# How many raw weight tiles may be held: a fixed number for each mode, or the pages that each unit leaves free

## The chip, the cores and the metric

The kernel runs on one core of a Trainium2 chip. The metric is the device time of one execution in microseconds (us), taken as the median of several runs. Engines are named as in the profile: PE is the matrix engine (PEld its weight loads), DVE the vector engine, ACT the scalar engine, POOL the general engine, SP the engine that only issues transfers; a q behind a name means its sequencer or its queue.

## The reference, cut to what matters

The kernel computes one layer over 256 positions of width 2048, all in float32: a SwiGLU feed-forward block, a mixer, a second feed-forward block, and a gated input at the end, with a layer norm behind each of the first three.

```python
def _swiglu(x, w1, w3, w2):
    return (jax.nn.silu(x @ w1) * (x @ w3)) @ w2
...
    merged = jax.nn.sigmoid(ga) * (y_m @ w_up_m) + jax.nn.sigmoid(gb) * (y_sb @ w_up_sb)
    return merged @ w_out
...
    for i in range(DEPTH):
        x = _layer_norm(ALPHA * x + 0.5 * _swiglu(x, ffn1_w1[i], ffn1_w3[i], ffn1_w2[i]), ln1_g[i], ln1_b[i])
        mix = _hybrid_mixer(x, w_in[i], b_gates_m[i], conv_m[i], norm_m[i], w_up_m[i], w_up_sb[i], w_out[i])
        x = _layer_norm(ALPHA * x + mix, ln2_g[i], ln2_b[i])
        x = _layer_norm(ALPHA * x + 0.5 * _swiglu(x, ffn2_w1[i], ffn2_w3[i], ffn2_w2[i]), ln3_g[i], ln3_b[i])
        x = x + jax.nn.sigmoid(x @ w_ple_gate[i]) * (p[i] @ w_ple_proj[i])
```

In the mixer, `ga` and `gb` (the two branch gates), the mLSTM's inputs and the attention's inputs are columns of one product `x @ w_in`. Nearly all the time is in these matrix products: 256 rows against weights that are read from memory once.

## The kernel before, in words

**Weights.** A weight tile is 256 rows by 512 columns, 512 KB. It is loaded by SP as a raw tile of one page (128 partitions, 2 x 512 float32). Then it is split into two float32r halves, of one page each: ACT casts it (hi, line 1277), DVE subtracts the cast from it (lo, line 1281). PE needs three matmuls for each product: activation hi by weight hi (line 1333), hi by lo (1334), lo by hi (1335). A **unit** is one weight tile against 128 positions, six matmuls.

**Seven products.** Where two column blocks of weights meet the same input, `seven` (line 356) replaces the eight block products of a 2 x 2 by 2 x 2 scheme by seven, with sums of weight tiles. A sum is made in the raw tile itself, by DVE (`plus`, line 373) or by a second transfer that adds to what is there (`plus_load`, line 379, issued by POOL). Such an adding transfer can start only when the raw tile has landed and the split of its earlier content has read it. One pair of column blocks has 28 units and 16 raw tiles; the four raw tiles b11 are held from the first units to the last, since each is changed three times.

**Order of work.** `program` is a list of units written out in advance; `weave` (line 168) mixes a main row of plain units with a side row of seven-product units. In each feed-forward block nine of the eleven column chunks are on the side; in the mixer there are six pairs: one for the attention's values, one for a gate of the mLSTM, and four for the branch gates (lines 1114 to 1115, `pair(g)`), which write into `gt` (line 1097). The main row there goes from the attention inputs over `half(0, 0)` and `half(1, 0)` (up-projection of the mLSTM branch, w_up_m) to the part called late (line 1112), which begins with `half(0, 1)` (attention branch, w_up_sb). The products of `half` end in line 1073. `Sched` runs the small work (transposes, activations, attention steps) at due times between the units.

**Pages.** One pool of 51 pages (`PAGES`) holds raw tiles, splits and nearly everything else: residuals (`big`, line 228), transposed activations (`act_tile`, line 231), attention tiles. A new tile takes the page of an earlier one, and its first writer waits until the last reader of that earlier tile is through.

**How far ahead.** The loop over `program` (line 1315) emits a unit, lets the small work run, and calls `splits_due` (line 1292), which emits the split of the next weight as long as fewer splits than the mode's second number are held. Each split gives back the raw tiles that it was the last to need, and `loads` (line 1242) then issues further raw loads as long as fewer than the mode's first number are held:

```python
HELD = {"ffn": (11, 6), "mix": (6, 6), "woven": (9, 6), "wide": (11, 6), "late": (8, 5)}
```

The mode "ffn" holds in the feed-forward blocks, "woven", "wide" and "late" in the woven part of the mixer one after the other, "mix" elsewhere. Within 6 weights of a stage boundary the numbers are 4 and 11. These are counts in the order of emission; SP, ACT, DVE and PE work through their own lists, so that SP can be well ahead of the splits that were emitted before its loads.

Of the kernel before, what the change touches and what calls it, by code (L numbers as in the profile page):

```python
# [24 lines left out]

PAGES = 51
TEMP_BUFS = 6


HELD = {"ffn": (11, 6), "mix": (6, 6), "woven": (9, 6), "wide": (11, 6), "late": (8, 5)}  # L30
RAW_EDGE, SPLIT_EDGE = 4, 11
EDGE = 6

# [1 line left out]
PSUM_BUFS = 8  # L35
# [151 lines left out]
    return [p[0] for p in pairs] + [p[1] for p in pairs]  # L187


@with_exitstack  # L190
def kernel(
    ctx: ExitStack,
    tc: tile.TileContext,
    x, p, ffn1_w1, ffn1_w3, ffn1_w2, ln1_g, ln1_b, w_in, b_gates_m, conv_m, norm_m,
    w_up_m, w_up_sb, w_out, ln2_g, ln2_b, ffn2_w1, ffn2_w3, ffn2_w2, ln3_g, ln3_b,
    w_ple_gate, w_ple_proj, out,
):
    nc = tc.nc
# [4 lines left out]
    consts = ctx.enter_context(tc.tile_pool(name="consts", bufs=1))  # L203
    dram_pool = ctx.enter_context(tc.tile_pool(name="dram", bufs=1, space=bass.MemoryType.DRAM))
    page_pool = ctx.enter_context(tc.tile_pool(name="page", bufs=PAGES))
    temp_pool = ctx.enter_context(tc.tile_pool(name="temp", bufs=TEMP_BUFS))
    small = ctx.enter_context(tc.tile_pool(name="small", bufs=4))
    ps_pool = ctx.enter_context(tc.tile_pool(name="ps", bufs=PSUM_BUFS, space=bass.MemoryType.PSUM))
    ctx.enter_context(tc.manual_schedule())

    sched = Sched()
    temps = [0]
# [49 lines left out]
    def load_x(c, t):  # L262
        nc.sync.dma_start(out=xres(t, c * COL), in_=x[t * P:(t + 1) * P, c * COL:(c + 1) * COL])
# [844 lines left out]
    last = sb(14, 15)  # L1108
# [3 lines left out]
    late = [Mode("late")] + half(0, 1, True) + half(1, 1, True) + ups(2)  # L1112
# [126 lines left out]
    def pieces(j):  # L1239
        return [slice(0, 1), slice(1, 2)] if j == 0 else [slice(0, 2)]  # L1240

    def loads(most=len(raws)):
        while pos["load"] < most and pos["raw"] < (4 if pos["at"] < 6 else limits(pos["split"])[0]):
            j = pos["load"]
            r = raws[j]
            r.tile = page_pool.tile([P, 2, COL], F32, name="raw", tag="page")
            for ks in pieces(j):
                at = 0
                for src in r.src:
                    n = src.shape[-1]  # L1250
                    nc.sync.dma_start(out=r.tile[:, ks, at:at + n], in_=src[:, ks])
# [16 lines left out]
    def split_one():  # L1268
        j = pos["split"]
        w = weights[j]  # L1270
        make(j)
        assert w.made or not w.make
        r = w.raw.tile[:, :, :w.cols]
        splits[j] = [page_pool.tile([P, 2, COL], F32R, name="split", tag="page") for _ in range(2)]
        hi, lo = (h[:, :, :w.cols] for h in splits[j])
        for ks in pieces(j):
            nc.scalar.copy(hi[:, ks], r[:, ks])  # L1277
# [3 lines left out]
            nc.vector.tensor_tensor(out=lo[:, ks], in0=r[:, ks], in1=hi[:, ks], op=ALU.subtract)  # L1281
        pos["split"] += 1
        for f in w.soon:
            assert f.raw.tile is not None
            f.make()
            f.made = True
        pos["raw"] -= len(w.frees)
        for r in w.frees:
            r.tile = None
        loads()  # L1290

    def splits_due():
        most = pos["at"] + 3 if pos["at"] < 8 else len(weights)
        while pos["split"] < most and len(splits) < limits(pos["split"])[1]:
            split_one()
            if at_edge(pos["split"]):
                break

    for c in range(4):
        if c == 0:  # L1300
            load_x(0, 0)
            loads(1)
        for t in range(TT):
            if c:
                load_x(c, t)
            sched.spawn(start(c, t), max(0.01 * t, 5.2 * c + 1.3 * t - 2.6))
        loads(2 * c + 2)
    sched.run()
    split_one()
    sched.now = 0.02  # L1310
    sched.run()
    splits_due()
    warm(WARM2)
    make_tri()
    for u in program:
        if isinstance(u, (Boundary, Mode)):
            continue
# [12 lines left out]
        for k in range(2):  # L1330
            hi, lo = a[:, 0, u.sub + k], a[:, 1, u.sub + k]
            first, last = u.start and k == 0, u.stop and k == 1
            nc.tensor.matmul(ps, hi, w[0][:, k, :u.cols], start=first, stop=False, skip_group_check=u.onto)  # L1333
            nc.tensor.matmul(ps, hi, w[1][:, k, :u.cols], start=False, stop=False, skip_group_check=u.onto)  # L1334
            nc.tensor.matmul(ps, lo, w[0][:, k, :u.cols], start=False, stop=last, skip_group_check=u.onto)  # L1335
# [35 lines left out]
```

## Time and profile before

| what | us |
|---|---|
| median of 3 runs | 2166.78 |
| lowest, highest of them | 2165.8, 2167.62 |
| the profiled execution | 2172.74 |
| its span, first to last instruction | 2171.1 |
| PE busy in it | 2154.1 |
| DVE busy | 1921.2 |
| ACT busy | 1360.8 |

The profile shows one execution. Busy time of PE is the union of its matmuls, whose ends are modelled, so small losses between matmuls lie inside it; idle time of PE is what is left of the span. A row of the windows view gives one stretch: its length, then busy time and number of instructions of PE, PEld, DVE, ACT and POOL, the granted clock of PE, the share of the DMA engines' time in use, and GB/s. A row of the waits view names who sat idle, what ended it, the total, the number of times and the longest. A number in brackets at the end of a timeline row is the idle time just before it, and what ended it.

### The profile page before, as it was taken

To read this page: it belongs to the slowest core of one execution; us is meant where nothing else is said; L and a number is where in the kernel's file an instruction comes from. 1 tells how busy PE (TensorE), PEld (TensorE's weight loads), DVE (VectorE), ACT (ScalarE), POOL (GpSimd) and SP (SyncE) were. 2 spreads that over 40 slices of the span, in tenths; PEclk is the share of its full clock that TensorE was granted. 3 is DMA by queue.
4 is the path that set the end of the run, shared out by engine and by line. 5 is a ranking of instruction groups with operands and counts; after the bars stand their busy time and mean duration, and the time that the engine had idled before them with its cause. 6 is when DMAs were issued, how large, how long until landed. Compare 5 with 4: busy or idle time off the path is not lost.

```text
span 2171.1 us, 27709 instructions
## 1 busy us (share of the span) xinstructions
PE 2154.1 (99%) x9774; PEld 1778.0 (82%) x9774; DVE 1921.2 (88%) x2122; ACT 1360.8 (63%) x1681; POOL 227.8 (10%) x194
## 2 busy tenths in 40 slices
PE   9999999999999999999999999999999999999999
PEld 7888888888888888888877888888888888887887
DVE  6899999999998898889889886799999999999974
ACT  7656666656665766678876563655656666556572
POOL 0111111111100000101110100011111111110000
PEclk9999999999999999999999999999999999999999
DMA  9899899999994667998988986679999999999642
GB/s 348 215 276 270 249 270 273 277 273 265 276 316 134 218 218 215 239 254 244 286 238 210 303 296 206 203 193 270 270 246 271 279 274 272 251 271 291 238 158 94
DMA packets 285355, 540.16 MB, mean 249 GB/s; under 512 B 17272, under 2 KB 34592, under 8 KB 285216
## 3 DMA queue, kind: packets, MB, share of 16 engines
q1 hardware_dynamic: 234624, 440.87, 59.8%
q0 software_dynamic: 50592, 97.53, 25.1%
q8 instruction: 76, 1.25, 0.2%
q14 instruction: 63, 0.52, 0.1%
HBM read 532.04 MB, written 6.29 MB: 248 GB/s over the span
## 4 chain that ended last, share of the span: by engine, by line
PE 87%; DVE 5%; DMA 3%; issue 3%; ACT 1%; POOL 0%; SPq 0%; DVEq 0%; POOLq 0%; ACTq 0%
PE mm L1334 28%; PE mm L1333 28%; PE mm L1335 28%; DMA raw<-in_ffn_w_dram 3%; DVE split L1281 3%; PE ms L300 1%; DVE raw L373 1%; ACT split L1277 1%; PE ms L526 0%; DVE temp L599 0%; POOL raw L379 0%; PE ms L913 0%; PE ms L928 0%; DVE big L651 0%; PE ms L991 0%
## 5 line engine op out<-in xcount | busy, mean ns | idle before, releaser
L1277 ACT CAST split<-raw 128x1024 fp32r<-128x1024 f32 (+1 forms) x1101 | 1099.4, 1043 | 538.4 <-DMA raw<-in_ffn_w_dram 194.2
L1281 DVE TENSOR_TENSOR split<-raw,split 128x1024 fp32r<-128x1024 f32 (+1 forms) x1101 | 1289.4, 1210 | 120.9 <-ACT split L1277 112.0
L1333 PE MATMUL mm<-split,actT 128*128 128x512 f32 (+1 forms) x3056 | 1199.2, 392 | 1.5 <-DVE big L427 1.4
L1334 PE MATMUL mm<-split,actT 128*128 128x512 f32 (+1 forms) x3056 | 1185.3, 388 | 4.2 <-DVE split L1281 4.2
L1335 PE MATMUL mm<-split,actT 128*128 128x512 f32 (+1 forms) x3056 | 1185.8, 388 | 0.6 <-DVE actT L307 0.6
L1334 PEld LDWEIGHTS mm<-split,actT 128*128 128x128 f32 x3056 | 574.9, 188 | 121.4 <-DVE split L1281 9.1
L1335 PEld LDWEIGHTS mm<-split,actT 128*128 128x128 f32 x3056 | 574.3, 188 | 120.8 <-DVE actT L307 1.4
L1333 PEld LDWEIGHTS mm<-split,actT 128*128 128x128 f32 x3056 | 574.8, 188 | 116.7 <-DVE big L427 1.6
L379 POOL DMA_DIRECT2D raw<-in_ffn_w_dram x140 | 169.8, 1439 | 1187.1 <-DVE split L1281 852.9
L373 DVE TENSOR_TENSOR raw<-raw 128x1024 f32<-128x1024 f32 x198 | 241.0, 1218 | 3.1 <-DMA raw<-in_w_in_dram 1.5
L379 POOL DMA_DIRECT2D raw<-in_w_in_dram x46 | 55.7, 1402 | 517.8 <-DVE split L1281 425.7
L651 DVE SCALAR_TENSOR_TENSOR big<-mm,big 128x512 f32<-128x512 f32 x112 | 76.2, 682 | 3.0 <-PE mm L1335 2.8
L302 ACT CAST actT<-ms 128x512 fp32r<-128x512 f32 x60 | 35.2, 587 | 66.8 <-PE ms L300 61.8
L599 DVE TENSOR_TENSOR temp<-mm,temp 128x512 f32<-128x512 f32 x108 | 73.0, 686 | 1.8 <-PE mm L1335 0.6
L307 DVE TENSOR_TENSOR actT<-ms,actT 128x512 fp32r<-128x512 f32 x60 | 41.0, 684 | 16.0 <-ACT big L306 11.6
L245 ACT ACTIVATE temp<-mm 128x512 f32<-128x512 f32 (+1 forms) x36 | 20.3, 570 | 48.2 <-PE mm L1335 48.2
L241 ACT ACT_TABLE_LOAD x34 | 43.6, 1283 | 0.6
L295 DVE TENSOR_TENSOR actT<-temp,actT 128x512 fp32r<-128x512 f32 x40 | 26.5, 687 | 17.4 <-ACT actT L294 17.3
L1193 DVE TENSOR_TENSOR temp<-temp,big 128x512 f32<-128x512 f32 (+1 forms) x10 | 5.8, 583 | 26.4 <-ACT temp L245 26.4
L294 ACT CAST actT<-temp 128x512 fp32r<-128x512 f32 x40 | 23.9, 620 | 8.0 <-DVE temp L318 7.4
L300 PEld LDWEIGHTS ms<-ident,temp 128*128 128x128 f32 x176 | 21.4, 140 | 8.0 <-DVE actT L307 2.9
L245 ACT ACTIVATE rstd<-mv,eps 128x1 f32<-128x1 f32 x6 | 1.8, 295 | 41.8 <-DVE mv L509 41.8
(137 smaller groups left out, 602.5 us busy)
## 6 DMA issues: line engine op xcount, KB each, us to landing
raw<-in_ffn_w_dram SPq DMA_DIRECT2D x527, 512.0 KB, 6.4
raw<-in_w_in_dram SPq DMA_DIRECT2D x144, 512.0 KB, 5.5
raw<-in_ffn_w_dram POOLq DMA_DIRECT2D x140, 512.0 KB, 10.1
raw<-in_w_in_dram POOLq DMA_DIRECT2D x46, 512.0 KB, 9.0
raw<-in_w_out_dram SPq DMA_DIRECT2D x32, 512.0 KB, 5.1
raw<-in_w_ple_gate_dram SPq DMA_DIRECT2D x32, 512.0 KB, 5.0
raw<-in_w_in_dram SPq DMA_DIRECT2D x56, 256.0 KB, 5.2
raw<-in_w_up_m_dram SPq DMA_DIRECT2D x16, 512.0 KB, 5.2
```

The source lines that it names most:

```text
L241: nc.scalar.preload_act_table_set(table[0])
L300: nc.tensor.transpose(ps[:, k], src[:, k * P:(k + 1) * P], ident[:])
L307: nc.vector.tensor_tensor(out=dst[:, 1], in0=ps[:], in1=dst[:, 0], op=ALU.subtract)
L373: nc.vector.tensor_tensor(out=out.tile[:, :, :cols], in0=a.tile[:, :, :cols], in1=b.tile[:, :, :cols], op=ALU.add)
L379: nc.gpsimd.dma_start(out=out.tile[:, :, :cols], in_=src, accum_op=ALU.add)
L599: nc.vector.tensor_tensor(out=out, in0=a, in1=b, op=op)
L651: nc.vector.scalar_tensor_tensor(out=xs, in0=ps, scalar=0.5, in1=xs, op0=ALU.mult, op1=ALU.add)
L1277: nc.scalar.copy(hi[:, ks], r[:, ks])
L1281: nc.vector.tensor_tensor(out=lo[:, ks], in0=r[:, ks], in1=hi[:, ks], op=ALU.subtract)
L1333: nc.tensor.matmul(ps, hi, w[0][:, k, :u.cols], start=first, stop=False, skip_group_check=u.onto)
L1334: nc.tensor.matmul(ps, hi, w[1][:, k, :u.cols], start=False, stop=False, skip_group_check=u.onto)
L1335: nc.tensor.matmul(ps, lo, w[0][:, k, :u.cols], start=False, stop=last, skip_group_check=u.onto)
```

## The change

The first numbers of four modes become 16, and the second number of "late" becomes 6; what really limits raw tiles and splits is now worked out from free pages. For that the function that emits the layer runs twice. The first run is a stand-in: its engines and pools do nothing, except that every page that is not a raw tile or a split notes the first and the last unit at which an instruction names it. `settle` then counts for each unit the pages in use, takes the most over the unit before, the unit itself and the three after it, and keeps 51 less that as the unit's room. The second run emits the real instructions. In it, `loads` stops from five raw tiles on when the raw tiles and twice the splits (those held, or the mode's number of them if that is more) reach the room; `splits_due` makes no split for which the room has no two pages left.

```diff
-HELD = {"ffn": (11, 6), "mix": (6, 6), "woven": (9, 6), "wide": (11, 6), "late": (8, 5)}
+AHEAD_UNITS = 4
+HELD = {"ffn": (16, 6), "mix": (6, 6), "woven": (16, 6), "wide": (16, 6), "late": (16, 6)}
...
+    def touch(self, n):
+        first, _ = self.spans[n] or (self.unit, None)
+        self.spans[n] = first, self.unit
...
+    def settle(self, pool):
+        used = [0] * (self.unit + 4)
+        for first, last in self.spans:
+            for u in range(first, last + 1):
+                used[u] += 1
+        self.room = [PAGES - max(used[max(u - 1, 0):u + AHEAD_UNITS]) for u in range(self.unit + 1)]
+        self.pool, self.unit = pool, 0
+
+    def left(self):
+        return self.room[self.unit] if self.room else PAGES
...
+    pages = Pages()
+    layer(DryCore(pages), pages, *[DryPool() for _ in range(5)], *args)
...
+    pages.settle(pool)
+    layer(tc.nc, pages, consts, dram_pool, temp_pool, small, ps_pool, *args)
...
+    def full(more):
+        return pos["raw"] + 2 * len(splits) + more > page_pool.left()
+
     def loads(most=len(raws)):
         while pos["load"] < most and pos["raw"] < (4 if pos["at"] < 6 else limits(pos["split"])[0]):
+            if pos["raw"] >= 5 and pos["raw"] + 2 * max(len(splits), limits(pos["split"])[1]) >= page_pool.left():
+                break
...
-        while pos["split"] < most and len(splits) < limits(pos["split"])[1]:
+        while pos["split"] < most and len(splits) < limits(pos["split"])[1] and not full(2):
...
+        page_pool.unit += 1
```

No arithmetic on the chip changes, and no transfer, split or matmul is added or removed. What changes is where in SP's list each raw load stands, and where the splits stand in the lists of ACT and DVE.

More of the change, by code (lines that the diff above doesn't have):

```diff
@@ L187, in skewed, with __init__, __getitem__, _same @@
     return [p[0] for p in pairs] + [p[1] for p in pairs]
-@with_exitstack
-def kernel(
-    ctx: ExitStack,
-    tc: tile.TileContext,
+class Dry:
+    def __init__(self, page=None):
+        self.page = page
+    def __getitem__(self, _):
+        return self
+    def _same(self, *_, **__):
+        return self
+    rearrange = bitcast = broadcast_to = _same
+class DryPool:
+    def tile(self, *_, **__):
+        return Dry()
+class DryCore:
+    def __init__(self, pages):
+        self.pages = pages
+    def __getattr__(self, _):
+        return self
+    def __call__(self, *args, **named):
+        for a in (*args, *named.values()):
+            if isinstance(a, Dry) and a.page is not None:
+                self.pages.touch(a.page)
@@ new lines, with __init__, tile @@
+class Pages:
+    def __init__(self):
+        self.pool, self.unit, self.spans, self.room = None, 0, [], None
+    def touch(self, n):
+        first, _ = self.spans[n] or (self.unit, None)
+        self.spans[n] = first, self.unit
+    def tile(self, shape, dtype, name, tag):
+        if self.pool:
+            return self.pool.tile(shape, dtype, name=name, tag=tag)
+        if name in ("raw", "split"):
+            return Dry()
+        self.spans.append(None)
+        return Dry(len(self.spans) - 1)
+    def settle(self, pool):
[7 more added lines that the diff above has]
+        return self.room[self.unit] if self.room else PAGES
@@ new lines, with kernel @@
+@with_exitstack
+def kernel(ctx: ExitStack, tc: tile.TileContext, *args):
+    pages = Pages()
+    layer(DryCore(pages), pages, *[DryPool() for _ in range(5)], *args)
+    pool = ctx.enter_context(tc.tile_pool(name="page", bufs=PAGES))
+    consts = ctx.enter_context(tc.tile_pool(name="consts", bufs=1))
+    dram_pool = ctx.enter_context(tc.tile_pool(name="dram", bufs=1, space=bass.MemoryType.DRAM))
+    temp_pool = ctx.enter_context(tc.tile_pool(name="temp", bufs=TEMP_BUFS))
+    small = ctx.enter_context(tc.tile_pool(name="small", bufs=4))
+    ps_pool = ctx.enter_context(tc.tile_pool(name="ps", bufs=PSUM_BUFS, space=bass.MemoryType.PSUM))
+    ctx.enter_context(tc.manual_schedule())
+    pages.settle(pool)
+    layer(tc.nc, pages, consts, dram_pool, temp_pool, small, ps_pool, *args)
@@ L194, with layer @@
+def layer(
+    nc, page_pool, consts, dram_pool, temp_pool, small, ps_pool,
     x, p, ffn1_w1, ffn1_w3, ffn1_w2, ln1_g, ln1_b, w_in, b_gates_m, conv_m, norm_m,
@@ L197 @@
 ):
-    nc = tc.nc
     x, out = x[0], out[0]
@@ L201 @@
     w_in, w_out, w_up_m, w_up_sb = w_in[0], w_out[0], w_up_m[0], w_up_sb[0]
[L203 to L209, printed above, removed]
     sched = Sched()
```

## The prediction

> **What bounds the kernel now.** The page's first part comes first, because it says which engine a gain must come from.
>
> ```profile
> span 2171.1 us, 27709 instructions
> PE 2154.1 (99%) x9774; PEld 1778.0 (82%) x9774; DVE 1921.2 (88%) x2122; ACT 1360.8 (63%) x1681; POOL 227.8 (10%) x194
> ```
>
> PE works for all but 17 us of its span. The change takes no matmul away, so it can only win back time in which PE stands or runs slowly. The windows view, one row for each stage, says where that is.
>
> ```profile
> core 0: us, PE busy (x) PEld busy (x) DVE busy (x) ACT busy (x) POOL busy (x), PEclk, DMA share, GB/s
> 0.00:60.00 60.00, 57.33 (x254) 46.71 (x255) 42.17 (x56) 41.59 (x59) 3.56 (x9) 1.00 0.90 320
> 60.00:640.00 580.00, 579.75 (x2595) 479.41 (x2594) 545.19 (x538) 355.19 (x380) 82.35 (x68) 1.00 0.95 269
> 640.00:1026.00 386.00, 386.00 (x1809) 319.35 (x1809) 342.59 (x462) 268.81 (x399) 28.08 (x23) 1.00 0.77 224
> 1026.00:1080.00 54.00, 53.36 (x282) 45.59 (x281) 44.11 (x57) 45.26 (x71) 9.70 (x8) 1.00 0.98 258
> 1080.00:1134.00 54.00, 51.77 (x247) 42.54 (x247) 47.27 (x56) 39.78 (x58) 4.87 (x4) 1.00 0.89 268
> 1134.00:1188.00 54.00, 51.24 (x221) 41.52 (x220) 49.40 (x56) 35.93 (x43) 7.28 (x6) 0.97 0.75 197
> 1188.00:1300.00 112.00, 112.00 (x511) 92.69 (x510) 100.62 (x102) 71.19 (x81) 7.15 (x6) 1.00 0.95 298
> 1300.00:1404.00 104.00, 104.00 (x474) 85.56 (x473) 65.37 (x83) 52.19 (x78) 0.00 (x0) 1.00 0.61 204
> 1404.00:2010.00 606.00, 602.56 (x2687) 495.95 (x2687) 567.74 (x571) 365.04 (x393) 84.86 (x70) 1.00 0.93 262
> 2010.00:2171.00 161.00, 156.06 (x709) 128.68 (x707) 116.71 (x147) 85.86 (x124) 0.00 (x0) 1.00 0.46 161
> ```
>
> PE idles 2.67 us at the start and 4.94 us at the end, which the change doesn't touch. In the first feed-forward block it idles 0.25 us, in the second 3.44 us. In the mixer, from 1026 to 1188, it idles 0.64 + 2.23 + 2.76 = 5.63 us, and in the last of these rows the clock is 0.97: another 1.6 us of the 54. So 7.25 us lie in the mixer and 3.69 us in the feed-forward blocks: 10.9 us, 0.5% of the time, is **all that can be won**.
>
> What does PE wait for in the mixer? Its own timeline shows the two longest gaps and the slow clock; the waits view from 1080 to 1160 shows what stands behind them.
>
> ```profile
> 1099.65 0.50 PE L1333 MATMUL mm<-split,actT 128*128 128x512 f32 x1 [1.38 <-DVE big L427]
> ...
> 1152.91 0.89 PE L1021 MATMUL ms<-temp,big 128*128 128x256 f32 x4 [2.00 <-DVE temp L1012]
> ...
> 1154.29 0.63 PE L1335 MATMUL mm<-split,actT 128*128 128x512 f32 x1
> ...
> 1157.75 0.40 PE L1335 MATMUL mm<-split,actT 128*128 128x512 f32 x1
> ```
>
> ```profile
> POOL raw L379 <- DMA raw<-in_w_up_sb_dram: 14.1, 1, 14.1
> DVE split L1281 <- ACT split L1277: 10.7, 7, 2.9
> ACT split L1277 <- PE mm L1334: 5.3, 4, 2.3
> ...
> ACT split L1277 <- PE mm L1335: 4.1, 2, 2.2
> ...
> ACT split L1277 <- DMA raw<-in_w_in_dram: 2.2, 1, 2.2
> ...
> ACT split L1277 <- PE ms L1010: 1.3, 1, 1.3
> ```
>
> Before a split ACT waits for PE: 5.3 + 4.1 + 1.3 = 10.7 us in 80. A cast reads a raw tile and writes a fresh page, and PE reads no raw tile. So it waits for a page that PE has not let go. DVE then waits 10.7 us for ACT, and behind these splits in DVE's list stand L427 and L1012, for which PE waits. **The splits lack pages.** The raw tiles don't: SP's list shows when the first weight of `half(0, 1)` was issued, DVE's when the product before it ended.
>
> ```profile
> 1133.93 4.42 SPq L1251 DMA_DIRECT2D raw<-in_w_up_sb_dram  x2
> ```
>
> ```profile
> 1162.56 0.69 DVE L1073 TENSOR_TENSOR big<-mm,big 128x512 f32<-128x512 f32 x1
> ```
>
> That raw tile was asked for 28 us before PE could use it, while a load lands within 6.4 us (an issues row below).
>
> **The change, part by part.** First the room. From the code, the pages that are neither raw nor split at about 1120 us are: x1T 8, its forms 8, `sv` 2, `ymT` brought back 4, `ysbT` 4, `gt` of two gates 4, an attention tile or two. That is 30 or 31, which leaves 20 or 21. "wide" asks for 11 + 2 x 6 = 23, so two or three pages are short. SP, which is ahead, has taken its eleven raw tiles; the splits get what is left, four of six. With the change the raw tiles stop at 20 - 12 = 8, and the six splits fit.
>
> From `half(0, 1)` on, "late" asks for 8 + 2 x 5 = 18. In use are 28 to 32, so room is for 7 to 11 raw tiles and six splits. The stretch from 1188 to 1300 runs the fourth pair of branch gates with these numbers and loses 0.00 us in 112. This is the nearest row for eight raw tiles: they are enough where the splits have room. It bounds the gain in the mixer from above at all 7.25 us. From below: the short pages are not the cause, and nothing is gained.
>
> I go gap by gap. The 1.38 us at 1099.65 goes: ACT's list has the page waits just ahead of it.
>
> ```profile
> 1098.09 1.04 ACT L1277 CAST split<-raw 128x1024 fp32r<-128x1024 f32 x1 [1.29 <-PE ms L1010]
> 1101.34 1.06 ACT L1277 CAST split<-raw 128x1024 fp32r<-128x1024 f32 x1 [2.21 <-PE mm L1335]
> ...
> 1107.69 1.28 ACT L241 ACT_TABLE_LOAD   x1
> ...
> 1111.09 1.28 ACT L241 ACT_TABLE_LOAD   x1
> ```
>
> The rest of that stretch, 2.23 - 1.38 = 0.85 us, and of the next, 2.76 - 2.00 = 0.76 us, lies near table loads of ACT of 1.28 us each. Two more splits in hand cover some of it; I take half, 0.8 us. The 2.00 us at 1152.91 ends a wait of ACT for an adding transfer; without the page waits ACT and DVE would reach this point some us earlier. I let it go, and with it the slow clock. The steps at 1154 take 0.63 us against 0.40. The 0.64 us before 1080 stays. Sum: 1.38 + 0.8 + 2.0 + 1.6 = **5.8 us**.
>
> The Trainium skill, "TensorE: Matmul & The Clock Gate", Part 1, has the clock halve after an idle window of about 3.4 us. Here the slow steps follow a gap of 2.0 us, so the row decides. If the slow steps had another cause than this gap, 1.6 us would stay and the sum be 4.2.
>
> Now the feed-forward blocks. In use are residuals 4, xT 8, its forms 8, and 2 for each hidden chunk that waits for its down-projection, one to four chunks: 22 to 28. At 28 the old 11 + 12 = 23 fits exactly. At 22 six pages lie free, and the change fills them: 13 to 16 raw tiles, back to 11 at the peaks. Does PE gain by that? The waits views of the two blocks (60 to 640, then 1404 to 2010) and the page's DMA parts answer.
>
> ```profile
> ACT split L1277 <- DMA raw<-in_ffn_w_dram: 90.1, 45, 4.2
> ...
> ACT split L1277 <- PE mm L1335: 12.9, 17, 2.9
> ACT split L1277 <- PE mm L1334: 11.9, 13, 1.7
> ```
>
> ```profile
> ACT split L1277 <- DMA raw<-in_ffn_w_dram: 102.0, 50, 4.0
> ```
>
> ```profile
> q1 hardware_dynamic: 234624, 440.87, 59.8%
> q0 software_dynamic: 50592, 97.53, 25.1%
> ...
> raw<-in_ffn_w_dram SPq DMA_DIRECT2D x527, 512.0 KB, 6.4
> ...
> raw<-in_ffn_w_dram POOLq DMA_DIRECT2D x140, 512.0 KB, 10.1
> ```
>
> ```profile
> 1945.01 12.16 DMA raw<-in_ffn_w_dram
> 1957.27 1.06 ACT split L1277
> ```
>
> ACT does wait for transfers, 192 us in all. The last fence, from the chain that ended last, tells which ones: the 12.16 us before ACT's split is the length of an adding transfer (POOL's, 10.1), not of a load (SP's, 6.4). Such a transfer starts when a split has read the raw tile, however many others are held. So more raw tiles bring nothing: I take **0**, between -3.69 us (the gaps go anyhow) and the loss in the rival below. The pages that are no longer spare cost ACT waits for PE; it has 24.8 us of them already in the first block, where PE loses 0.25.
>
> Smaller edits go at nothing. The stand-in emits no instruction. SP's loads move behind `bring_ym_back` and `bring_back`, transfers that stood behind blocked loads and now go sooner. POOL's list keeps its order; its wait of 14.1 us for a landing raw tile shows what would be hurt first if eight were too few. A split that is held back is emitted later; it is no wait, and nothing queues behind it on ACT or DVE. At the boundaries raw tiles stop at five while eleven splits are held. From 1300 to 1404 PE doesn't idle now, and DVE is busy 65 us of 104; this slack is the cover, and I take 0.
>
> So the profiled execution would take 2172.74 - 5.8 = 2166.9 us. It lies 5.96 us above the median, 2166.78; carried over, the median becomes 2166.78 - 5.8 = **2161.0 us**.
>
> **The rivals.** *It doesn't reach PE.* PE's gaps would come from ACT's own bursts (table loads, sigmoids, attention), and pages only decide where ACT waits. For it: PE loses nothing in the first feed-forward block, although ACT waits 24.8 us for pages there. Against it: those 24.8 us are spread over 580, the 10.7 us over 80. Then 0 to 1 us is won: 2166 us.
>
> *Everything goes.* The deeper stock also smooths the second feed-forward block: 2166.78 - 10.9 = 2155.9 us. For it: nearly the same block lost 0.25 us the first time. Against it: its waits are for adding transfers.
>
> *Bursts of loads delay the adding transfers*, and it ends slower. A down pair frees four hidden pages at once, and four raw loads follow together. Before, the count of eleven held them back. A load takes 440.87 MB in 59.8% of 2171.1 us, so 1.54 us of all DMA engines for 512 KB; four take 6.2 us. An adding transfer in flight shares the engines and lands up to half of that later, 3.1 us. DVE idles only 580 - 545.19 = 34.8 us of 580, 1.0 us in the 16 of such a burst. So PE loses up to 2.1 us each time, and with four such steps in each block 8 x 2.1 = 17 us: 2166.78 - 5.8 + 17 = 2178 us. It decides once the lateness passes DVE's 1.0 us. For it: adding transfers land after 8.5 us where the DMA share is lower.
>
> ```profile
> raw<-in_w_in_dram POOLq DMA_DIRECT2D x8, 512.0 KB, 8.5
> ```
>
> That is 1080 to 1160, against 10.1 in the feed-forward blocks. Against it: waits of up to 4.2 us cost PE 0.25 us in the first block.
>
> The Trainium skill, "DMA: Bandwidth & Descriptors", section "Queues, rings and completion order", says that each engine takes turns, packet by packet, between the queues that have work. By that rule a longer queue of SP takes no more turns from POOL's than a short one that is never empty. At a DMA share of 0.95 it is seldom empty, so the 17 us would shrink to about 5% of them, 0.9 us. No row here shows the turns themselves.
>
> **How the numbers follow.** A measurement of this kernel can tell about 0.2%, 4.3 us, from no change: faster means below 2162.4, slower above 2171.1. The forecast has 0.45, with a range of its own from 2157.5 to 2165, two thirds of it below 2162.4 (0.30 and 0.15). Everything goes: 0.10, faster. It doesn't reach PE: 0.21, of which 0.19 is the same and 0.02 slower. The bursts: 0.24, its price anywhere from a third to the whole, so 0.22 slower and 0.02 the same. Together 0.40 faster, 0.36 the same, 0.24 slower. The range goes from 2156, everything gone, to 2175, which takes in the lower half of the bursts.
>
> **What would show it.** Right: from 1026 to 1188 PE idles under 3 us, the clock is 1.00 in every row, and ACT's waits for PE before a split fall well below 10.7 us there. ACT waits for no load of SP. The feed-forward rows stay at 0.3 and 3 to 4 us idle, and adding transfers land in about 10 us. Wrong: ACT waits for loads in the mixer (eight raw tiles were too few), or adding transfers land after 11 us or more with a feed-forward row that loses several us more, or the mixer's gaps stand where they are with the page waits gone.

## The result and the profile after

| kernel | median, us | lowest to highest, us | runs |
|---|---|---|---|
| before | 2167.47 | 2165.8 to 2170.44 | 10 |
| after the change | 2172.91 | 2169.7 to 2175.22 | 10 |

The ratio is 1.0023, 95% interval 1.0014 to 1.0033: the change makes the kernel **slower by about 5 us**. The forecast was 5.8 us faster.

The profiled execution of the kernel before that the prediction worked from took 2172.74 us, more than any timed run beside it. The first experiment below profiled the same kernel once more: 2168.69 us, span 2167.0, inside the range of its timed runs (2165.07 to 2169.77). That second profile is the base of all comparisons from here on; its windows view:

```profile
60.00:640.00 580.00, 580.00 (x2599) 480.25 (x2598) 546.45 (x540) 357.49 (x382) 82.34 (x68) 1.00 0.96 270
640.00:1026.00 386.00, 386.00 (x1810) 319.44 (x1809) 342.33 (x461) 268.64 (x399) 28.08 (x23) 1.00 0.77 222
1026.00:1188.00 162.00, 156.37 (x746) 129.71 (x745) 140.78 (x169) 120.22 (x169) 21.84 (x18) 0.99 0.89 242
...
1404.00:2010.00 606.00, 604.09 (x2701) 499.07 (x2700) 570.99 (x575) 370.11 (x397) 84.86 (x70) 1.00 0.94 265
```

The same view of the changed kernel, whose profiled execution took 2173.0 us:

```profile
60.00:640.00 580.00, 578.12 (x2582) 476.61 (x2580) 542.43 (x535) 359.43 (x380) 82.34 (x68) 1.00 0.95 268
640.00:1026.00 386.00, 384.94 (x1803) 318.50 (x1804) 342.87 (x458) 266.79 (x389) 28.08 (x23) 1.00 0.75 218
1026.00:1080.00 54.00, 52.64 (x270) 44.61 (x269) 44.96 (x60) 45.25 (x75) 9.70 (x8) 1.00 0.98 275
1080.00:1134.00 54.00, 52.82 (x262) 43.76 (x260) 48.16 (x57) 42.28 (x63) 4.87 (x4) 1.00 0.81 225
1134.00:1188.00 54.00, 51.97 (x225) 42.26 (x225) 48.69 (x57) 36.83 (x44) 7.28 (x6) 0.97 0.87 242
1188.00:1300.00 112.00, 111.02 (x506) 91.70 (x505) 100.75 (x104) 70.23 (x79) 7.22 (x6) 1.00 0.93 290
1404.00:2010.00 606.00, 604.05 (x2702) 499.30 (x2701) 572.68 (x575) 371.48 (x396) 84.85 (x70) 1.00 0.94 265
```

Look at the first row of each. In the first feed-forward block PE idled 0 us and now idles 1.88, and it gets through 2582 matmuls in place of 2599. A matmul takes 580 / 2599 = 0.223 us there, so the 17 are 3.8 us: the stops of PE are partly too short to show as idle time. At the boundary to the mixer it loses another 1.06 us (640 to 1026). From 1026 to 1188 it idles 1.36 + 1.18 + 2.03 = 4.57 us where it idled 5.63: 1.06 us won, not 5.8, and the clock of 0.97 is still there. From 1188 to 1300, where nothing was lost, 0.98 us is. The second feed-forward block takes as long as it did. So the change wins a microsecond in the mixer, gives it back a hundred microseconds later, and loses 3.8 + 1.06 = 4.9 us in the first feed-forward block and at its end. Together that is 4.8 us; the medians differ by 5.4, the two profiled spans by 2171.0 - 2167.0 = 4.0, because the changed kernel's profile is 0.8 us ahead at 60 us, which one execution can't tell from chance.

What changed there? The waits view of the changed kernel from 60 to 640. The lines have moved in the changed kernel: 1354 is ACT's split, 1358 DVE's, 1410 to 1412 are PE's three matmuls, 451 the adding transfer.

```profile
ACT split L1354 <- DMA raw<-in_ffn_w_dram: 57.6, 29, 3.9
...
ACT split L1354 <- PE mm L1411: 44.2, 42, 3.6
...
ACT split L1354 <- PE mm L1412: 27.9, 30, 3.0
...
PEld mm L1411 <- DVE split L1358: 3.1, 5, 1.1
```

The same view of the kernel before, in its second profile:

```profile
ACT split L1277 <- DMA raw<-in_ffn_w_dram: 78.5, 43, 4.6
...
ACT split L1277 <- PE mm L1334: 19.5, 22, 1.7
...
ACT split L1277 <- PE mm L1335: 10.9, 19, 1.7
```

ACT waits less for transfers, as one would wish (57.6 us, before 78.5). Matched cast by cast with the order in the program, all of the 78.5 us and 54 of the 57.6 are waits for adding transfers, not for loads of SP. But it waits 44.2 + 27.9 = 72.1 us for PE to let go of a page; before it was 30.4. And PE now waits for DVE's half of a split, a row that the second profile of before doesn't have in this block. How such a stop comes about, the timeline of the changed kernel shows (ACT, DVE and PE rows, sorted by start):

```profile
585.69 1.05 ACT L1354 CAST split<-raw 128x1024 fp32r<-128x1024 f32 x1 [3.86 <-DMA raw<-in_ffn_w_dram]
589.69 1.05 ACT L1354 CAST split<-raw 128x1024 fp32r<-128x1024 f32 x1 [2.95 <-DMA raw<-in_ffn_w_dram]
...
590.77 1.22 DVE L1358 TENSOR_TENSOR split<-raw,split 128x1024 fp32r<-128x1024 f32 x1 [1.03 <-ACT split L1354]
...
590.79 0.50 PE L1410 MATMUL mm<-split,actT 128*128 128x512 f32 x1 [0.31 <-ACT split L1354]
...
592.05 0.50 PE L1411 MATMUL mm<-split,actT 128*128 128x512 f32 x1 [0.76 <-DVE split L1358]
```

Two splits in a row wait 3.86 and 2.95 us for an adding transfer. The kernel before has waits of up to 4.6 us of this kind and loses nothing by them, because finished splits lie ready. Here there is none left, and PE starts on each half as it is made.

**Pages, counted.** From the trace I counted what is on the chip between 240 and 400 us. A raw tile counts from the issue of its load to the end of DVE's last split that reads it; a split (two pages) from the start of ACT's cast to the end of the last matmul that reads it; "ready" are splits that DVE has finished and PE has not begun. The lead is the median time from the issue of a raw tile's load to its first split. The kernels with a number are the experiments below.

| kernel | raw tiles | splits | pages of both | ready | lead, us | ratio to before |
|---|---|---|---|---|---|---|
| before, (11, 6) | 12.4 | 5.9 | 24.2 | 2.5 | 20 | 0.9999 |
| the change | 14.3 | 4.9 | 24.1 | 1.6 | 26 | 1.0023 |
| room less 4 (5) | 11.0 | 5.5 | 22.0 | 1.9 | 16 | 1.0010 |
| (15, 6) (6) | 16.1 | 4.4 | 24.9 | 1.1 | 31 | 1.0077 |
| (9, 7) (7) | 10.4 | 6.7 | 23.8 | 3.3 | 14 | 1.0054 |
| four pages away (8) | 12.1 | 4.4 | 20.9 | 1.1 | 20 | 1.0064 |
| (9, 6) (9) | 10.8 | 6.0 | 22.8 | 2.5 | 15 | 0.9993 |
| second limit off (11) | 14.2 | 5.2 | 24.5 | 1.9 | 25 | 1.0033 |
| (13, 6) (12) | 14.4 | 4.9 | 24.2 | 1.6 | 25 | 1.0018 |

The first two rows are the result in short: the same 24 pages, two more of them with raw tiles, two fewer with splits.

Where in the first block is the time lost? Set matmul against matmul, the changed kernel falls behind the second profile of before by 1.1 us between 240 and 400 us and by 3.9 between 560 and 640, and hardly anywhere else in the block. In these last 80 us the raw tiles rise from 14.0 to 17.6, the splits fall from 5.6 to 4.7, the ready ones from 1.9 to 1.1. ACT waits 7.3 us for pages of PE there, before not at all; but the eight adding transfers also land later there, 11.0 us after their issue at the median instead of 10.1. So pages are short and transfers late at once, and no run tells the two shares of these 3.9 us apart. The feed-forward part alone (experiment 2) loses 1.7 us there with its adding transfers at 10.2.

In the second block the splits fall as well, from 5.6 to 5.1 (1404 to 2010 us), and ACT's page waits rise from 31.0 to 54.0 us; yet it loses no more than the second profile of before. A smaller stock makes a stop likelier; it doesn't set its price.

### The profile page after: what moved, and what is told of

Read it like the earlier page. It is cut to its first block, busy times and chain, and to the rows that moved or that the text cites. A ratio compares the mean times of both kernels' runs of the same rounds, so it can differ in the third digit from the quotient of the medians.

```text
span 2171.0 us, 27878 instructions
## 1 busy us (share of the span) xinstructions
PE 2152.6 (99%) x9774; PEld 1777.8 (82%) x9774; DVE 1924.7 (89%) x2122; ACT 1372.9 (63%) x1681; POOL 227.9 (10%) x194
## 4 chain that ended last, share of the span: by engine, by line
PE 87%; issue 4%; DVE 3%; DMA 3%; ACT 1%; POOL 1%; SPq 0%; DVEq 0%; POOLq 0%; ACTq 0%
PE mm L1411 28%; PE mm L1410 28%; PE mm L1412 28%; DMA raw<-in_ffn_w_dram 3%; DVE split L1358 2%; PE ms L372 1%; ACT split L1354 1%; DVE raw L445 1%; POOL raw L451 1%; PE ms L598 0%; PE ms L1093 0%; PE ms L985 0%; PE ms L1000 0%; ACT L313 0%; DVE big L499 0%
## 5 line engine op out<-in xcount | busy, mean ns | idle before, releaser
L1208 DVE SCALAR_TENSOR_TENSOR big<-big,mm 128x512 f32<-128x512 f32 x8 | 5.5, 686 | 25.3 <-PE mm L1412 25.3
```

## The experiments

All were run five rounds against the kernel before; intervals are 95%.

**1 to 4: which part.** The first is the kernel before once more, to see what a repetition differs by.

> The kernel before, unchanged: a second profiled execution of it, and the floor of the comparison. Every theory expects a ratio of 1.000 with an interval of about 0.001 to either side. The first profiled execution took 2172.74 us, above all ten timed ones (2165.8 to 2170.44); if that was a chance of that one execution, this profile lies near 2167 and shows less idle PE than 14 us outside the start and the end; if profiling costs this kernel 5 us, it lies near 2172 again.

Measured: 0.9999 (0.999 to 1.0008), and the second profile above.

The second has the change in the feed-forward blocks only: `left()` answers "no limit" in the other modes, and they keep their old numbers. The third has it in the mixer only, with the feed-forward blocks as before.

```diff
+    def left():
+        return 2 * PAGES if [m for e, m in modes if e <= pos["split"]][-1] in ("woven", "wide", "late") else page_pool.left()
...
-HELD = {"ffn": (16, 6), "mix": (6, 6), "woven": (16, 6), "wide": (16, 6), "late": (16, 6)}
+HELD = {"ffn": (16, 6), "mix": (6, 6), "woven": (9, 6), "wide": (11, 6), "late": (8, 5)}
```

> Only the feed-forward part of the change: mode ffn holds up to 16 raw tiles within the room; woven, wide and late keep 9, 11 and 8 raw tiles with 6, 6 and 5 splits and know no room. Theory F (the loss comes from the feed-forward blocks, where no page stays free and ACT waits for PE's pages before its casts): 2173, ratio 1.002 to 1.003. Theory M (the loss comes from the mixer, where fewer raw tiles are held than before): 2167, ratio 1.000. Theory N (no one part: any new order of the same work moves the time by some us): anywhere from 0.998 to 1.003.

> Only the mixer's part: mode ffn keeps 11 raw tiles and 6 splits and knows no room; woven, wide and late hold up to 16 and 6 within the room. Theory F: 2165 to 2168, ratio 0.999 to 1.000 (a little gain in the mixer is possible). Theory M: 2173, ratio 1.002 to 1.003. Theory N: anywhere from 0.998 to 1.003.

The fourth is the change with the old table: the room only takes away, it never lets more raw tiles in.

```diff
-HELD = {"ffn": (16, 6), "mix": (6, 6), "woven": (16, 6), "wide": (16, 6), "late": (16, 6)}
+HELD = {"ffn": (11, 6), "mix": (6, 6), "woven": (9, 6), "wide": (11, 6), "late": (8, 5)}
```

> The room stays everywhere, but only as a further limit: the modes keep their old numbers (11, 9, 11 and 8 raw tiles; late with 5 splits). So no mode holds more than before, and wide holds less. Theory F: 2167, ratio 1.000, since the feed-forward blocks keep their free pages. Theory M: 2172 or more, ratio 1.002, since the mixer's raw tiles are cut as in the change. Theory N: anywhere from 0.998 to 1.003.

Measured: feed-forward only 1.0018 (1.0009 to 1.0027), mixer only 1.0001 (0.9992 to 1.001), old table 1.0002 (0.9993 to 1.001). The windows and waits of the feed-forward part alone, where 1357 is ACT's split and 1414 and 1415 are PE's second and third matmul:

```profile
60.00:640.00 580.00, 578.40 (x2587) 477.54 (x2586) 544.95 (x537) 359.09 (x380) 82.35 (x68) 1.00 0.96 269
```

```profile
ACT split L1357 <- PE mm L1414: 49.8, 49, 3.6
...
ACT split L1357 <- PE mm L1415: 24.4, 27, 3.0
```

PE's 1.60 us of idle time and ACT's 74.2 us of page waits come with the raw tiles in the feed-forward blocks. The mixer's part alone is neutral, and its windows say why:

```profile
1026.00:1188.00 162.00, 157.04 (x749) 130.05 (x748) 142.85 (x171) 122.06 (x171) 21.84 (x18) 0.99 0.91 252
...
1188.00:1300.00 112.00, 111.02 (x506) 91.71 (x505) 99.11 (x100) 72.08 (x81) 7.18 (x6) 1.00 0.92 293
```

It wins 157.04 - 156.37 = 0.67 us from 1026 to 1188 and loses 0.98 from 1188 to 1300. With the old table that loss doesn't come.

**5 to 8: is it the pages, or the early loads?** The fifth counts four pages less room in the feed-forward blocks. The sixth and seventh are the kernel before with other fixed numbers, without any count of room. The eighth is the kernel before with four pages taken out of use during the woven part of each feed-forward block; POOL writes one column of each at its start and its end, and loads are issued as before.

```diff
+    def left():
+        return page_pool.left() - 4 * ([m for e, m in modes if e <= pos["split"]][-1] == "ffn")
```

```diff
-HELD = {"ffn": (11, 6), ...
+HELD = {"ffn": (15, 6), ...
```

```diff
-HELD = {"ffn": (11, 6), ...
+HELD = {"ffn": (9, 7), ...
```

```diff
+        def take():
+            kept.extend(big() for _ in range(4))
+            for k in kept:
+                nc.gpsimd.memset(k[:, 0:1], 0.0)
...
+        program.append(take)
+        program.extend(weave(main[HEAD:], side))
+        program.append(give)
```

> The change, but in mode ffn the room counts four pages less, so that about 7 to 13 raw tiles are held there instead of 11 to 16; the raw loads still follow the room in jumps. Theory P (raw tiles that SP issues ahead of their turn take the pages of the splits, so that PE has fewer finished splits in hand): ratio 0.999 to 1.000, and splits held on the chip in the first block go from about 5.0 back to 5.9. Theory B (the jumps in the loads delay the adding transfers): the jumps stay, ratio 1.001 to 1.002.

> The kernel before with one number changed: mode ffn holds 15 raw tiles instead of 11, always; no room, no holding back of splits. Theory P: slower, ratio 1.002 to 1.004, since 15 + 12 and up to 28 pages of other tiles are more than 51 and the splits come short. Theory B: 1.000, since a fixed number has no jumps. A third theory, S (the change loses because it holds splits back by its own rule): 1.000, since nothing is held back here.

> The kernel before with mode ffn at 9 raw tiles and 7 splits instead of 11 and 6: the same 23 pages, two raw tiles given for one split. Theory P: a raw tile is now asked for some 20 us before its split, more than it needs, so the trade is free and one more split in hand helps: ratio 0.998 to 1.000. If raw tiles are what feeds PE (the reason for the change): slower, 1.001 or more, with ACT waiting for loads of SP.

> The kernel before, with four pages of the pool taken by tiles that nothing uses, from the start of each feed-forward block's woven part to its end (POOL writes one column of each at both ends: eight small writes a block that the layer doesn't need). Raw tiles stay at 11 and splits at 6. Theory P: slower, 1.002 to 1.004, because pages are short though no load is earlier. Theory B and theory S: 1.000.

Measured: room less four 1.001 (1.0001 to 1.0019), (15, 6) 1.0077 (1.0065 to 1.009), (9, 7) 1.0054 (1.0042 to 1.0067), four pages away 1.0064 (1.0052 to 1.0077). The row of the first block and ACT's page waits, first with (15, 6), then with four pages away (its ACT split is line 1291, its matmuls 1348 and 1349):

```profile
60.00:640.00 580.00, 576.06 (x2570) 473.86 (x2569) 540.74 (x532) 356.65 (x377) 82.34 (x68) 1.00 0.95 265
```

```profile
ACT split L1277 <- PE mm L1334: 37.0, 43, 3.1
...
ACT split L1277 <- PE mm L1335: 29.1, 36, 3.3
```

```profile
60.00:640.00 580.00, 575.39 (x2562) 472.02 (x2561) 539.34 (x531) 357.59 (x377) 82.65 (x73) 1.00 0.95 264
```

```profile
ACT split L1291 <- PE mm L1349: 31.1, 38, 3.1
ACT split L1291 <- PE mm L1348: 27.9, 37, 2.0
```

These two tell pages and early loads apart. With four pages away the loads lead by 20 us, as before, and the raw tiles are no more than before; but splits are down to 4.4, as with (15, 6), and PE loses about the same, 4.61 us of idle time against 3.94. **Missing pages are enough for such a loss, without any load that comes early.** Not all of it is a missing split: of the waits of PE and its weight loads in this block about half with four pages away, and somewhat less than half with (15, 6), stand before the transposes (line 300), whose operands DVE makes in between the delayed splits.

With four pages less counted, ACT's page waits fall to 8.7 + 7.9 = 16.6 us and about half of the loss goes, 1.0010 after 1.0023, though the two intervals overlap. The splits come back to 5.5, not to the 5.9 that theory P expected, and 1.001 lies at the lower end of theory B's range. So this run alone doesn't exclude that jumps in the loads have a share in the change's loss; (15, 6), (13, 6) and the four pages, which have no such jumps, show that the loss doesn't need them.

The seventh is a miss: with fewer raw tiles and more splits than before, and with no wait of PE for a split in the first block, it is slower by 0.54%. Its waits and its timeline around the longest stop:

```profile
PEld ms L300 <- DVE actT L307: 4.0, 4, 1.4
```

```profile
348.01 1.23 DVE L373 TENSOR_TENSOR raw<-raw 128x1024 f32<-128x1024 f32 x1 [2.44 <-DMA raw<-in_ffn_w_dram]
349.16 1.22 DVE L1281 TENSOR_TENSOR split<-raw,split 128x1024 fp32r<-128x1024 f32 x1
350.29 0.68 DVE L651 SCALAR_TENSOR_TENSOR big<-mm,big 128x512 f32<-128x512 f32 x1
...
351.03 0.66 PE L300 MATMUL ms<-ident,temp 128*128 128x128 f32 x4 [1.52 <-DVE big L651]
```

PE waits not for a split but for the work behind one. DVE stands 2.44 us before a sum of raw tiles, works through it and a split, and only then takes up line 651, for which PE's transpose has waited 1.52 us. Nine raw tiles or seven splits, which of the two puts that work behind the wait? That was left to the ninth.

**9 to 11.** The ninth is (9, 6).

```diff
-HELD = {"ffn": (11, 6), ...
+HELD = {"ffn": (9, 6), ...
```

> The kernel before with (9, 6) in the feed-forward blocks: nine raw tiles and six splits as before; the earlier run with (9, 7) was slower by 0.54%, with no split ever wanting, and its lost time stood in three or four gaps of 0.85 to 1.7 us ahead of the transposes. Theory Q (the seventh split is the cause: ACT and DVE work through one more split ahead of the copies of the transposes, and PE waits for these): with six splits the gaps ahead of the transposes go, PE is busy for 579 to 580 of the 580 us from 60 to 640, and the time is 2166 to 2169. Theory R (nine raw tiles are too few, loads come late): PE loses as in the run with (9, 7), about 4 us from 60 to 640, ACT waits for raw tiles' DMAs over 100 us there, and the time is 2175 to 2180.

Measured: 0.9993 (0.9984 to 1.0002). The first block's row, and the second's:

```profile
60.00:640.00 580.00, 580.00 (x2598) 480.66 (x2597) 546.59 (x539) 354.19 (x381) 82.34 (x68) 1.00 0.96 270
...
1404.00:2010.00 606.00, 606.00 (x2713) 502.20 (x2712) 574.92 (x579) 369.16 (x400) 84.85 (x70) 1.00 0.95 267
```

It loses nothing in either block. So nine raw tiles are enough, with a lead of 15 us, and the seventh split is what cost the 0.54%. By the timeline above this would be one more split, and the wait before it, emitted ahead of the short work in DVE's list; one stop shows it, the others were not followed. (9, 6) has the lowest time of all kernels here, but its interval reaches over 1: no gain over before can be claimed.

The tenth tests the prediction's reason for the mixer: at most seven raw tiles in "woven" and "wide", without any count of room.

```diff
-HELD = {..., "woven": (9, 6), "wide": (11, 6), ...
+HELD = {..., "woven": (7, 6), "wide": (7, 6), ...
```

> The kernel before with at most 7 raw tiles, not 9 and 11, in the two gate parts of the mixer: the raw tiles that crowd out the splits between 1026 and 1188 are fewer than the change makes them. Theory G (the prediction's: the squeezed splits cost PE there 5.63 us of idle time and the slow clock after it): PE's idle time from 1026 to 1188 falls below 3 us, the splits held rise to five or more, and the time is 2160 to 2163. Theory N (the gaps there are not for splits): the splits held rise but the idle time stays at 4.5 to 6 us, and the time is 2166 to 2168. Theory L (seven raw tiles are too few for the loads): PE loses more than before in 640 to 1188, ACT waits longer for raw tiles' DMAs, and the time is 2170 to 2180.

Measured: 1.0016 (1.0007 to 1.0025), slower. The raw tiles between 1020 and 1160 us fall from 12.1 to 9.2, and ACT's waits for PE before a split, from 1026 to 1188, from 10.4 + 5.0 to 2.2 + 1.4 us; but the splits on the chip stay at 4.7. That is neither theory G nor theory N, which both have the splits rise. The time lies in the range of theory L, and ACT does wait 4.8 us for loads of w_up_m there, for which it didn't wait before. PE's timeline in the second profile of before shows the four longest gaps that this stretch had:

```profile
1098.63 0.50 PE L1333 MATMUL mm<-split,actT 128*128 128x512 f32 x1 [1.38 <-DVE big L427]
...
1114.80 0.50 PE L1334 MATMUL mm<-split,actT 128*128 128x512 f32 x1 [0.73 <-DVE split L1281]
...
1135.53 0.50 PE L1334 MATMUL mm<-split,actT 128*128 128x512 f32 x1 [0.76 <-DVE split L1281]
...
1151.91 0.89 PE L1021 MATMUL ms<-temp,big 128*128 128x256 f32 x4 [1.99 <-DVE temp L1012]
```

and with seven raw tiles:

```profile
1101.98 0.51 PE L1333 MATMUL mm<-split,actT 128*128 128x512 f32 x1 [2.21 <-DVE big L427]
...
1138.38 0.51 PE L1334 MATMUL mm<-split,actT 128*128 128x512 f32 x1 [0.38 <-DVE split L1281]
...
1155.96 0.92 PE L1021 MATMUL ms<-temp,big 128*128 128x256 f32 x4 [3.20 <-DVE temp L1012]
```

Only 0.73 + 0.76 = 1.49 us stood before splits, and of that 0.38 is left. The two longest gaps stand before steps of the attention and of the gates (lines 427 and 1012), and they grow although the page waits are nearly gone. The changed kernel, which doesn't cut the raw tiles as far, has for the same two lines (now 499 and 1084):

```profile
1102.25 0.50 PE L1410 MATMUL mm<-split,actT 128*128 128x512 f32 x1 [0.15 <-DVE big L499]
...
1154.92 1.43 PE L1093 MATMUL ms<-temp,big 128*128 128x256 f32 x3 [1.93 <-DVE temp L1084]
```

The first gap is nearly gone in it (0.56 us stand before a second step of the same line), the second is not, although ACT has no page wait at all between 1096 and 1156. DVE's own list shows what the second one waits for. In the second profile of before DVE stops last at 1134.25 us and then works without a stop through sums, splits and short steps until line 1012 is done at 1151.76: it is busy for 13.47 of the 13.5 us from 1138 to 1151.5. ACT's last page wait lies 30 us ahead of the gap, at 1121. In the changed kernel DVE works just as long without a stop, from 1137.35 on. With seven raw tiles it stops once in between, for 1.06 us, and the gap is 1.2 us longer. **The second gap is DVE's own work, not a wait for pages.**

The eleventh is the change without its second limit, so that a split is never held back by the count.

```diff
-        while pos["split"] < most and len(splits) < limits(pos["split"])[1] and not full(2):
+        while pos["split"] < most and len(splits) < limits(pos["split"])[1]:
```

> The change without its second limit: raw tiles still follow the free pages, but a split is no longer held back when raw tiles and splits by count fill the pages. Theory P (SP issues loads ahead of the splits emitted before them, and so takes the pages meant for splits): nothing changes, the time is 2170 to 2174, PE is busy for 578 to 579 of the 580 us from 60 to 640, and ACT's splits wait for PE's pages for over 60 us there. Theory H (the second limit holds the splits back itself): without it the splits come as in the kernel before, the time is 2166 to 2168, and ACT's splits wait for PE for about 30 us.

Measured: 1.0033 (1.002 to 1.0045). PE is busy 578.38 of the 580 us, ACT waits 83.2 us for pages of PE. The median, 2174.87, lies just above theory P's range. The splits rise a little, from 4.9 to 5.2, but the loss stays, so it is not this limit that makes it.

**12: how the loss grows.** (13, 6), fixed.

```diff
-HELD = {"ffn": (11, 6), ...
+HELD = {"ffn": (13, 6), ...
```

> The kernel before with (13, 6) in the feed-forward blocks, fixed, with no room counted: between (11, 6), which is the kernel before, and (15, 6), which was slower by 0.77%. Theory P (each raw tile more takes a page from the splits once the pages are full, and PE pays only where no finished split is left): the raw tiles on chip rise by about two, ACT's splits wait for PE's pages between 30 us (before) and 66 us (with 15) from 60 to 640, and the loss lies between, most of it where the other pages are most: 2169 to 2178. Theory E (early loads themselves harm, pages or not): the loss is half that of (15, 6) with ACT's waits for PE as before, 2173 to 2176. Theory N: no loss, 2165 to 2168.

Measured: 1.0018 (1.0009 to 1.0028), 2171.31 us. The waits view:

```profile
ACT split L1277 <- PE mm L1334: 24.0, 33, 3.2
ACT split L1277 <- PE mm L1335: 20.9, 28, 3.2
```

44.9 us of page waits lie between 30.4 and 66.1. Without any count of room it holds as many raw tiles and splits between 240 and 400 us as the change (14.4 and 4.9), and its ratio is about the same. The places are not: its profile loses 1.7 us there, nothing from 560 to 640, and 2.5 in the second block. From 9 to 11 raw tiles the time doesn't change, two more cost 0.2%, four more 0.8%.

## Why the prediction was wrong

**What bounds the kernel** held: PE is busy for 99% of the span after as before. But its base was one execution that took longer than the timed ones: of the 3.44 us in the second feed-forward block the second profile shows 1.91, and (9, 6) none. One reading was loose: "a load lands within 6.4 us" takes a median for a bound (the longest between 1080 and 1160 us took 9.1), which a lead of 28 us can bear.

**The step that failed first** is the feed-forward sum: "At 22 six pages lie free, and the change fills them", "So more raw tiles bring nothing", valued at 0, and the cover for it, "The pages that are no longer spare cost ACT waits for PE; it has 24.8 us of them already in the first block, where PE loses 0.25." That more raw tiles gain nothing is right: 9 serve as well as 11. The term that was set at nothing is what the change costs. That the change fills free pages is right where the other pages are few: from 60 to 240 us raw tiles rise from 13.2 to 16.8, splits fall only from 6.0 to 5.6, and no time is lost. Between 240 and 400 us, however, raw tiles and splits held 24.2 pages before, and no kernel here holds more than 24.9, so hardly a page was spare: 1.9 more raw tiles took the place of one split. Over the block ACT's page waits went from 30.4 to 72.1 us, the finished splits fell from 2.5 to 1.6, and then the waits for adding transfers, which had cost nothing, reached PE: 4.9 us where the prediction has 0. The 24.8 us were read as a proof that page waits are free. They were free only while finished splits covered them, and it is this cover that the change spent. The prediction asked what happens without cover for the smaller edits, not for this one.

Why doesn't the count prevent it? It keeps twelve pages for six splits in the order of emission. Emitting a split gives its raw tile back in the count, and the next load follows at once. SP's list runs ahead: the load takes its page some 26 us before its split (before: 20), while the raw tile given back still lies on the chip until ACT and DVE have come to it. So 14.3 raw tiles are there and the splits find 4.9 places. Experiment 8 shows that missing pages have such a price without any early load; 11 that the limit on splits is not the cause; 5 that four pages of allowance take about half of the loss away. How much of the 3.9 us at the block's end belongs to the later adding transfers stays open.

**The mixer's 5.8 us** came to 1.06 from 1026 to 1188. Go through the sum term by term. The gap at line 427, 1.38 us, went down to 0.15 + 0.56; the short gaps before splits, taken at 0.8, from 1.49 to 0.48: 1.7 us of the 2.2 that these two terms promised. The 2.0 us at line 1012 and the 1.6 of the slow clock stayed, 1.93 us and a clock of 0.97. And one gap, before line 963, grew from 0.63 to 1.36 us.

The step that failed is "without the page waits ACT and DVE would reach this point some us earlier". Between 1096 and 1156 the raw tiles did fall as the prediction wanted, from 11.9 to 9.6, and ACT's 5.4 us of page waits there went to none. But the splits only rose from 3.8 to 4.1, with 43.9 of the 51 pages in use, and ahead of line 1012 DVE works without a stop, as shown at the tenth experiment. The room was counted too small as well: about 1120 us the first trace has 27 other pages between their first write and their last read, not 30 or 31. So **"The splits lack pages"** was true of ACT's waits and not of what holds PE at this line. What made the gap at line 427 shrink here and grow to 2.21 us with seven raw tiles no run separates: there ACT waits for loads of w_up_m (2.5 us at the longest) and DVE for a transfer of w_in (1.8 us) instead. And the stretch from 1188 to 1300, at no loss before, was taken to stay so with "7 to 11 raw tiles and six splits": there the new numbers cost 0.98 us, in the change and in the mixer's part alone, but not with the old table.

**The rivals.** "It doesn't reach PE" has the right size for the mixer, 0 to 1 us, but not the reason: the gap that stays stands behind DVE's work, not behind bursts of ACT. "Bursts of loads delay the adding transfers" had the right side, but its mechanism does not show over the whole kernel, and no row gives the 16 us that it takes for a burst. The issues part of the changed kernel's page (KB, then median us from issue to landing):

```profile
raw<-in_ffn_w_dram SPq DMA_DIRECT2D x527, 512.0 KB, 7.4
...
raw<-in_ffn_w_dram POOLq DMA_DIRECT2D x140, 512.0 KB, 9.8
```

SP's loads land later, after 7.4 us where it was 6.3 in the second profile of before, but the adding transfers after 9.8 as in that profile (10.1 in the first). Only in the last 80 us of the first block do they come later, 11.0 against 10.1. The Trainium skill ("DMA: Bandwidth & Descriptors", "Queues, rings and completion order") says that an engine takes turns between the queues that have work. If so, a longer queue delays mostly itself; these two rows agree, though no row shows the turns. The rival that was missing is the plain one: raw tiles and splits share the pages, and what one gains the other loses.

## What to carry to other kernels

Before pages are called spare, count what lies on the chip from issue to last read, not in the order of emission: a queue that only issues loads runs ahead, and room kept aside by a count is taken by whoever comes first in time. If one stage must not run short, give it buffers of its own. A wait that costs nothing is covered by a stock; ask of each change whether it draws on that stock. And a wait that stands just behind another in an engine's list is not yet caused by it: take the first away and see whether the second goes.

## What the runs showed of the hardware

The clock after a gap of about 2 us is a matter of chance. Thirteen profiles, of the two kernels and the experiments other than the tenth, have the mixer's longest gap at 1.9 to 2.1 us, where PE waits for line 1012. In nine of them a row of matmuls behind it starts 0.427 us apart in place of 0.227; in four none does. The nine list a mean clock of 0.999 for the whole execution, the four 1.000. One and the same program does either: of 85 timed runs of the kernel before, 67 list 0.999 and 18 list 1.000. After the gaps of 1.0 to 1.7 us no profile shows it; after the tenth's 2.21 and 3.20 us both times. The timeline of the tenth, behind its gap of 2.21 us:

```profile
1103.10 0.63 PE L1333 MATMUL mm<-split,actT 128*128 128x512 f32 x1
1103.52 0.63 PE L1334 MATMUL mm<-split,actT 128*128 128x512 f32 x1
```

and (9, 6) behind its gap of 2.00 us:

```profile
1153.76 0.39 PE L1333 MATMUL mm<-split,actT 128*128 128x512 f32 x1
1153.98 0.39 PE L1334 MATMUL mm<-split,actT 128*128 128x512 f32 x1
```

So the 1.6 us that the prediction tied to this gap are paid in most executions, not in each. The Trainium skill, "TensorE: Matmul & The Clock Gate", Part 1, describes a window of about 3.4 us that runs freely, whatever the kernel does. That the same gap is paid for in some executions and not in others would fit such a window; that a gap of 2.0 us is enough does not fit a whole window of idleness.
